# The first projection of a hybrid decoder trunk, issued in written order with the norm applied at eviction

## The chip, the cores and the metric

The kernel runs on one core of one Trainium2 chip. The metric is the device time of one execution in microseconds (us); three runs of the kernel before gave 558.02, 559.24 and 559.66 us, so the median is 559.24. The engines are named as the profile names them: PE (matrix multiplications, with PEld for its weight loads), DVE (element by element work, also the only one here that subtracts), ACT (functions, casts and scaled copies), POOL (memsets here) and SP, whose queue issues nearly every DMA.

## The reference, cut to what matters

Two layers, each of this form (x is 256 tokens by 1024):

```
for layer in range(2):
    h = rmsnorm(x, pre_norm[layer])            # x * rsqrt(mean(x*x) + eps) * g
    proj = h @ w_in[layer]                     # 1024 x 7704
    (hq, hf, hi, hz, nq, kc, vc, ks, vs, kw, vw, ng, nz) = split(proj)
    o_h = rmsnorm(hgrn2(hq, hf, hi), ...) * silu(hz)
    o_n = nsa(rope(nq), kc, vc, ks, vs, kw, vw, ng) * silu(nz)
    x = x + rmsnorm(concat(o_h, o_n) @ w_out[layer], post_norm[layer])
```

Only the start of layer 0 matters here: the norm of x, the product with the 1024 columns that give nq (the attention queries, scaled and rotated), and the handing over of the normalised x to the products that follow.

## The kernel before

**Precision.** Each float32 matrix is split into a high part (rounded to the fp32r type by an ACT cast) and a low part (DVE: the value minus its high part). A product is three matmuls: high by high, high by low, low by high.

**Tiles and units.** The tokens are two tiles of 128 (a = 0, 1). x is turned (transposed by PE, four 128x128 blocks per PSUM bank) so that the 1024 inputs lie on partitions in eight blocks; Hhi and Hlo hold its two parts. The weights come in units of 512 KB: one DMA into `raw` (five buffers), one ACT cast into `whi` (line 202), one DVE subtraction into `wlo` (line 203), eight buffers each. `Ring` issues the DMAs ahead of use; a DMA has to wait until the `raw` buffer that it writes has been read by line 203. Here w0, w1, ... are the units in the order of the plan. Units w0 to w7 make up the nq projection, w8 to w11 the next one (the forget gate of the first four heads, by `b_group`), and so on: w30 belongs to the third of the later groups (`kv_s`).

**The nq projection (a_pair, mm_a).** For each unit and each tile PE does six matmuls of 128x512: with weights of w and Hhi (line 368), w low and Hhi (369), w high and Hlo (370). The column group g = 0 uses w0 to w3, g = 1 uses w4 to w7. Tile 1 follows tile 0 by four units in layer 0. Three PSUM banks (`mmb`) hold the sums. When a sum is complete, `nq_evac` scales and rotates it (`rope`: one ACT op, four small DVE ops), and some microseconds later `turn_q` transposes the result (line 430).

**The norm (norm_in).** Per tile: ACT squares two halves of x (line 339), DVE adds the sums (341), ACT takes the root (331), DVE the reciprocal (332), DVE multiplies x by 1/rms and by g (344, g spread over the partitions by matmuls against a row of ones, line 1088), PE transposes (351), ACT and DVE split (355, 356).

**The order of work.** The instructions are recorded in program order and then placed on each engine by a scheduler; the functions given to `later` run when a counted PE time has passed, conversions of weights LAG = 9 us after their DMA is recorded. `consts2` loads the small constants (masks, biases, positions) and works out the forget gate's lower bound; before, it stands ahead of the layers. Each engine runs its instructions in order, each waiting for what it reads.

Of the kernel before, what the change touches and what calls it, by code (L numbers as in the profile page):

```python
# [10 lines left out]
F32 = mybir.dt.float32  # L11
# [84 lines left out]
def build(ctx, tc, A, out):  # L96
# [97 lines left out]
    class Ring:  # L194
        def __init__(self):
            self.made, self.taken, self.used = [], 0, 0
            self.split, self.lag = [], 0.0

        def convert(self, n):
            while len(self.split) < n:  # L200
                raw, hi, lo, shaped = self.made[len(self.split)]
                S.copy(out=hi, in_=raw)  # L202
                V.tensor_tensor(out=lo, in0=raw, in1=hi.bitcast(F32), op=OP.subtract)  # L203
                self.split.append((shaped(hi), shaped(lo)))

        def fill(self, n=RING):
            while len(self.made) < min(len(plan), self.used + n):
# [14 lines left out]
                if len(dims) == 3:  # L222
                    for a in range(dims[1]):
                        nc.sync.dma_start(out=shaped(raw)[:, :, a, :], in_=src[:, :, a, :])
                else:
                    nc.sync.dma_start(out=shaped(raw), in_=src)
                self.made.append((raw, hi, lo, shaped))
                if self.lag:
# [41 lines left out]
    def consts():  # L270
        nc.sync.dma_start(out=ct, in_=A["ct"])

    def consts2():
        rows = sp.tile([128, 128], F32, name="rows", tag="st", bufs=2)
        prow = sp.tile([128, 128], F32, name="prow", tag="st", bufs=2)
        m2 = sp.tile([128, 256], F32, name="m2", tag="st", bufs=2)
        nc.sync.dma_start(out=m2, in_=A["ct2"])
        nc.gpsimd.memset(cm3, 0.0)
        nc.gpsimd.memset(rows, 0.0)
# [6 lines left out]
        nc.gpsimd.memset(pat.rearrange("p (b t) -> p b t", t=32)[:, :, 0:1], 1.0)  # L286
        for i, nm in enumerate(("cmp_b1_k", "cmp_b1_v", "hgrn_out_norm")):
# [84 lines left out]

    def mm_b(ps, un, u, c):
# [49 lines left out]
    def nq_evac(a, g, ps):  # L423
        st = sp.tile([128, 4, 128], F32, name="st", tag="st", bufs=2)
        rope(st, ps.rearrange("p (h d) -> p h d", h=4), rope_q[a], 4, SCALE)
# [648 lines left out]

    def layers(general):
        ring = Ring()
        lm = None
        if not general:
            V.memset(eps_t, EPS)
            S.activation(out=eps_w, in_=eps_t, func=AF.Sqrt)  # L1080
        grow = slot("B0")[0:1, :D]
        ones = slot("B4")[0:1, 0:128]
        V.memset(ones, 1.0)
        nc.sync.dma_start(out=grow, in_=A["pre_norm"][0:1, :])
        xr = load_x(0, (0,), 2)
        gpre = [mmb(), mmb()]
        for q in range(2):
# [87 lines left out]
```

## Time and profile before

| | |
|---|---|
| median of 3 runs | 559.24 us |
| the profiled execution | 558.97 us |
| its span (first to last instruction) | 557.2 us |
| PE busy | 543.8 us (98%) |
| DVE busy | 398.8 us (72%) |
| ACT busy | 333.0 us (60%) |
| mean DMA rate | 173 GB/s |

The span is what the views below show; about 1.8 us of the execution lie around it. The busy times are shares of the whole span, so they say little of its first 40 us, which the change touches. A row of the timeline gives the start, the duration, the engine, the line of the kernel, the operation with the tile written and the tile read, its shape, and in square brackets how long the engine idled before it and which work ended that. Matmuls are pipelined: their pace is the distance of two starts, not the duration.

### The profile page before, as it was taken

To read this page: it belongs to the slowest core of one execution; us is meant where nothing else is said; L and a number is where in the kernel's file an instruction comes from. 1 tells how busy PE (TensorE), PEld (TensorE's weight loads), DVE (VectorE), ACT (ScalarE), POOL (GpSimd) and SP (SyncE) were. 2 spreads that over 40 slices of the span, in tenths; PEclk is the share of its full clock that TensorE was granted. 3 is DMA by queue.
4 is the path that set the end of the run, shared out by engine and by line. 5 is a ranking of instruction groups with operands and counts; after the bars stand their busy time and mean duration, and the time that the engine had idled before them with its cause. 6 is when DMAs were issued, how large, how long until landed. Compare 5 with 4: busy or idle time off the path is not lost.

```text
span 557.2 us, 9821 instructions
## 1 busy us (share of the span) xinstructions
PE 543.8 (98%) x3675; PEld 487.6 (88%) x3675; DVE 398.8 (72%) x883; ACT 333.0 (60%) x632; POOL 9.6 (2%) x18
## 2 busy tenths in 40 slices
PE   7999999999999999999999999989999999999994
PEld 4889998899888989988888999979988888898884
DVE  4887997889777277563687599888987654866422
ACT  6576537865567685562557763677646768746311
POOL 4000000000000001001000000000000000000000
PEclk9999999999999999999999999999999999999998
DMA  8698548965146158566385755697433622956111
GB/s 302 195 314 257 146 127 266 304 193 152 39 117 190 35 166 291 185 191 188 115 262 162 228 154 152 196 302 256 125 101 84 174 85 63 303 172 200 59 38 44
DMA packets 72197, 96.56 MB, mean 173 GB/s; under 512 B 3383, under 2 KB 49357, under 8 KB 72142
## 3 DMA queue, kind: packets, MB, share of 16 engines
q1 hardware_dynamic: 71854, 95.33, 55.2%
q8 instruction: 31, 0.51, 0.4%
q10 hardware_dynamic: 288, 0.52, 0.2%
q14 instruction: 24, 0.20, 0.1%
HBM read 93.75 MB, written 2.10 MB: 172 GB/s over the span
## 4 chain that ended last, share of the span: by engine, by line
PE 88%; DMA 4%; ACT 3%; DVE 2%; issue 1%; SPq 0%; ACTq 0%; DVEq 0%
PE ps_mm L378 10%; PE ps_mm L380 10%; PE ps_mm L379 10%; PE ps_mm L368 9%; PE ps_mm L369 9%; PE ps_mm L370 9%; PE ps_mm L1005 4%; PE ps_mm L1007 4%; PE ps_mm L1006 4%; DMA raw<-in_w_in 2%; ACT whi L202 2%; PE ps_t L668 2%; DMA raw<-in_cmp_w_v 2%; PE ps_s L608 1%; DVE wlo L203 1%
## 5 line engine op out<-in xcount | busy, mean ns | idle before, releaser
L203 DVE TENSOR_TENSOR wlo<-raw,whi 128x1024 fp32r<-128x1024 f32 (+1 forms) x168 | 203.0, 1223 | 60.7 <-ACT whi L202 56.3
L202 ACT CAST whi<-raw 128x1024 fp32r<-128x1024 f32 (+1 forms) x168 | 174.9, 1052 | 87.9 <-PE ps_mm L379 24.5
L378 PE MATMUL ps_mm<-Hhi,whi 128*128 128x256 f32 x448 | 127.5, 285 | 0.0
L380 PE MATMUL ps_mm<-Hhi,wlo 128*128 128x256 f32 x448 | 125.7, 281 | 0.0
L379 PE MATMUL ps_mm<-Hlo,whi 128*128 128x256 f32 x448 | 125.7, 281 | 0.0
L368 PE MATMUL ps_mm<-whi,Hhi 128*128 128x512 f32 (+1 forms) x256 | 102.0, 399 | 0.7 <-ACT Hhi L355 0.7
L370 PE MATMUL ps_mm<-whi,Hlo 128*128 128x512 f32 (+1 forms) x256 | 98.9, 386 | 0.0
L369 PE MATMUL ps_mm<-wlo,Hhi 128*128 128x512 f32 (+1 forms) x256 | 98.8, 386 | 0.0
L379 PEld LDWEIGHTS ps_mm<-Hlo,whi 128*128 128x128 f32 x448 | 84.5, 189 | 0.1
L378 PEld LDWEIGHTS ps_mm<-Hhi,whi 128*128 128x128 f32 x448 | 84.3, 188 | 0.1
L380 PEld LDWEIGHTS ps_mm<-Hhi,wlo 128*128 128x128 f32 x448 | 84.4, 188 | 0.0
L370 PEld LDWEIGHTS ps_mm<-whi,Hlo 128*128 128x128 f32 x256 | 48.7, 190 | 10.3 <-DVE Hlo L356 0.3
L368 PEld LDWEIGHTS ps_mm<-whi,Hhi 128*128 128x128 f32 x256 | 48.9, 191 | 8.5 <-ACT Hhi L355 1.1
L369 PEld LDWEIGHTS ps_mm<-wlo,Hhi 128*128 128x128 f32 x256 | 49.0, 191 | 7.5 <-DVE wlo L203 0.5
L630 ACT ACTIVATE sB<-ps_s,nm 128x256 f32<-128x256 f32 (+1 forms) x40 | 16.9, 428 | 12.2 <-DVE nm L627 11.5
L627 DVE CUSTOM_DVE_ANT_0 ps_s<-ps_s,cm 128x128 f32<-128x128 f32 (+1 forms) x64 | 22.4, 371 | 1.9 <-PE ps_s L610 0.7
L671 DVE TENSOR_TENSOR sB<-ps_t,sB 128x512 fp32r<-128x512 f32 x12 | 8.3, 688 | 20.1 <-ACT sB L670 20.1
L1005 PE MATMUL ps_mm<-whi,sN 128*128 128x512 f32 x48 | 19.0, 397 | 0.0
L1006 PE MATMUL ps_mm<-wlo,Hhi 128*128 128x512 f32 x48 | 18.9, 395 | 0.0
L1007 PE MATMUL ps_mm<-whi,Hlo 128*128 128x512 f32 x48 | 18.9, 395 | 0.0
L1006 PE MATMUL ps_mm<-wlo,sN 128*128 128x512 f32 x48 | 18.9, 394 | 0.0
L1007 PE MATMUL ps_mm<-whi,sN 128*128 128x512 f32 x48 | 18.9, 394 | 0.0
(299 smaller groups left out, 921.0 us busy)
## 6 DMA issues: line engine op xcount, KB each, us to landing
raw<-in_w_in SPq DMA_DIRECT2D x112, 512.0 KB, 4.5
raw<-in_w_out SPq DMA_DIRECT2D x32, 512.0 KB, 4.3
raw<-in_w_in SPq DMA_DIRECT2D x8, 536.0 KB, 4.1
raw<-in_cmp_w_k SPq DMA_DIRECT2D x16, 256.0 KB, 3.4
raw<-in_cmp_w_v SPq DMA_DIRECT2D x16, 256.0 KB, 3.2
sB<-in_x SPq DMA_DIRECT2D x3, 512.0 KB, 3.6
sB<-in_post_norm SPq DMA_DIRECT2D x2, 512.0 KB, 4.8
xs<-sB SPq DMA_DIRECT2D x4, 256.0 KB, 2.0
```

Of the source, the lines that this page charges most:

```text
L202: S.copy(out=hi, in_=raw)
L203: V.tensor_tensor(out=lo, in0=raw, in1=hi.bitcast(F32), op=OP.subtract)
L368: P.matmul(out=ps, lhsT=hh, rhs=wh, start=k == 0, stop=False)
L369: P.matmul(out=ps, lhsT=hh, rhs=wl, start=False, stop=False)
L370: P.matmul(out=ps, lhsT=hl, rhs=wh, start=False, stop=k == KT - 1)
L378: P.matmul(out=ps, lhsT=wh, rhs=hh, start=k == 0, stop=False)
L379: P.matmul(out=ps, lhsT=wh, rhs=hl, start=False, stop=False)
L380: P.matmul(out=ps, lhsT=wl, rhs=hh, start=False, stop=k == KT - 1)
L627: V.tensor_tensor_reduce(out=sb[b], in0=sb[b], in1=mk[b], scale=-1.0, scalar=3e38, op0=OP.add, op1=OP.min, accum_out=nm[:, i, b:b + 1])
L1005: P.matmul(out=ps, lhsT=hi, rhs=wh, start=first, stop=False)
L1006: P.matmul(out=ps, lhsT=hi, rhs=wl, start=False, stop=False)
L1007: P.matmul(out=ps, lhsT=lo, rhs=wh, start=False, stop=last)
```

## The change

The nq projection of layer 0 gets a function of its own, `first`, whose instructions stay on each engine in the order in which they are written.

- x is turned as it comes from memory. DVE multiplies it by g, which now lies one value per partition (`gcol`, turned from an 8x128 load), while it copies it out of PSUM (`whole`); ACT makes the high part (`top`), DVE the low part (`rest`).
- The sum of squares is taken later (`squares`), and 1/rms is applied to the finished sums: `stats` puts it into the table and the scale that `nq_evac` uses.
- For the later projections x needs the factor too: `spread` multiplies the turned x by 1/rms (spread along the tokens by a matmul of ones with a diagonal) and splits it again into Hhi and Hlo.
- Each unit is used by both tiles, one after the other; the last pair of matmuls of most units is the one with the low part of x.
- The first conversions are cut in halves; w0 and the x of tile 1 are loaded in two DMAs each; the first columns of the constants (the identity) and g are loaded by ACT's queue.
- PE multiplies zeros (`dummies`, 384 columns of bf16) eight times ahead of the first transposes and twice behind them.
- `consts2` moves behind the first forget gate group; its two transposes and small DVE operations come later.

```diff
     class Ring:
+        def high(self, i, s=slice(None)):
+            raw, hi, lo, shaped = self.made[i]
+            S.copy(out=hi[:, s], in_=raw[:, s])
+
+        def low(self, i, s=slice(None)):
+            raw, hi, lo, shaped = self.made[i]
+            V.tensor_tensor(out=lo[:, s], in0=raw[:, s], in1=hi[:, s].bitcast(F32), op=OP.subtract)
...
     def consts():
-        nc.sync.dma_start(out=ct, in_=A["ct"])
...
+        nc.sync.dma_start(out=ct[:, 128:], in_=A["ct"][:, 128:])
...
+    def mm_x(ps, un, u, H, order):
+        last = (u == KT // 2 - 1, order[-1], 1)
+        for j, kind in enumerate(order):
+            for i in range(2):
+                k = 2 * u + i
+                P.matmul(out=ps, lhsT=H[kind[0] == "l"][:, k, :], rhs=un[kind[1] == "l"][:, i, :],
+                         start=(u, j, i) == (0, 0, 0), stop=(True, kind, i) == last)
...
+    def first(ring, general):
...
+        def dummies(n):
+            if not general:
+                for i in range(n):
+                    P.matmul(out=wps[:, 0:384], lhsT=cm3[:, 0:128], rhs=cm3, start=True, stop=True)
...
+        def whole(a, k0, n):
+            ks, o = slice(k0, k0 + n), (k0 % 4) * 128
+            V.tensor_tensor(out=full[a][:, ks, :],
+                            in0=turned[a, k0 // 4][:, o:o + 128 * n].rearrange("p (k t) -> p k t", k=n),
+                            in1=gcol[:, ks, None].to_broadcast([128, n, 128]), op=OP.mult)
+
+        def top(a, k0, n):
+            S.copy(out=H[a][0][:, k0:k0 + n, :], in_=full[a][:, k0:k0 + n, :])
...
+        def stats(a, ss):
+            r = rstd_of(ss[:, 0:1], D, 1, "r1")
...
+            def spread():
+                rb = tb()
+                P.matmul(out=rb[:, 0:128], lhsT=ones, rhs=rd, start=True, stop=True)
+                V.tensor_tensor(out=full[a], in0=full[a], in1=rb[:, None, 0:128].to_broadcast([128, 8, 128]),
+                                op=OP.mult)
+                S.copy(out=Hhi[:, a], in_=full[a])
+                V.tensor_tensor(out=Hlo[:, a], in0=full[a], in1=Hhi[:, a].bitcast(F32), op=OP.subtract)
...
+            ring.fill(4)
...
+            dummies(8)
+            gp = sb_()
+            P.transpose(out=gp[:, 0:8], in_=grow, identity=ident[0:8, 0:8])
+            V.tensor_copy(out=gcol, in_=gp[:, 0:8])
+            turn_x(0)
+            dummies(2)
...
+            unit(0, 0)
+            turn_x(1)
+            ring.high(1)
+            ring.low(1)
+            ring.fill(7)
+            unit(0, 1)
+            ring.high(2)
+            whole(1, 0, 4)
+            top(1, 0, 4)
+            rest(0, 4, 4)
+            rest(1, 0, 4)
+            whole(1, 4, 4)
+            top(1, 4, 4)
+            ring.low(2)
+            ring.fill(8)
+            rest(1, 4, 4)
+            unit(1, 0, late)
+            unit(1, 1, late)
+            ring.high(3)
+            ring.low(3)
+            unit(0, 2, late)
+            done()
+            unit(1, 2, late)
+            s0 = squares(0)
+            ring.high(4)
+            ring.low(4)
...
+            spread = [stats(0, s0), stats(1, s1)]
+            evacuate(0, 0)
+            ring.high(6)
+            ring.low(6)
...
     def layers(general):
...
+            if l == 0:
+                first(ring, general)
+            else:
+                a_pair(ring, nq_evac, 8)
...
                     rests.append(hgrn_fast(l, c, ring))
+                    if (l, c) == (0, 0):
+                        consts2()
```

How the change moves instructions, at three places. The first is PE at the start of the program. Before (L1088 spreads g, L351 transposes the normalised x of tile 0, L368 to L370 are the matmuls of w0):

```order
L1088 MATMUL ps_mm<-sB_97,sB_98 128x512 x2
L351 MATMUL ps_t<-ct,sA_121 128x128 x8
L368 MATMUL ps_mm<-whi,Hhi 128x512
L369 MATMUL ps_mm<-wlo,Hhi 128x512
L370 MATMUL ps_mm<-whi,Hlo 128x512
```

The same place now, behind the first eight dummies (sA_95 and sA_96 are the high and low part of tile 0, sA_97 that of tile 1, sB_116 its x):

```order
L1201 MATMUL ps_s<-ct,sB_102 128x8
L1116 MATMUL ps_t<-ct,sB_108 128x128 x8
L1110 LDWEIGHTS cm_71
L1110 MATMUL ps_o<-cm_71 128x384
L1110 LDWEIGHTS cm_71
L1110 MATMUL ps_o<-cm_71 128x384
L394 MATMUL ps_mm<-whi,sA_95 128x512 x2
L394 MATMUL ps_mm<-whi,sA_96 128x512 x2
L394 MATMUL ps_mm<-wlo,sA_95 128x512 x2
L1116 MATMUL ps_t<-ct,sB_116 128x128 x8
L394 MATMUL ps_mm<-whi,sA_95 128x512 x2
L394 MATMUL ps_mm<-whi,sA_96 128x512 x2
```

The matmuls of w0 for tile 0 now stand ahead of tile 1's transposes, and all of PE's queue behind those waits for the x of tile 1, then for w1.

The second place is SP's queue at the start, before:

```order
L1084 DMA sB0_97<-in_pre_norm 1x1024
L157 DMA sB2_101<-in_x 128x512 x2
L271 DMA ct_70<-in_ct 128x544
L226 DMA raw_109<-in_w_in 128x2x512
L226 DMA raw_115<-in_w_in 128x2x512
L157 DMA sB3_145<-in_x 128x1024
L226 DMA raw_147<-in_w_in 128x2x512
```

and now, down to the masks (raw_111 is w0, raw_119 is w1, raw_271 is w9, m2_610 holds the masks):

```order
L157 DMA sB2_108<-in_x 128x512 x2
L237 DMA raw_111<-in_w_in 128x512 x2
L157 DMA sB3_116<-in_x 128x512 x2
L239 DMA raw_119<-in_w_in 128x2x512
L239 DMA raw_123<-in_w_in 128x2x512
L286 DMA ct_70<-in_ct 128x416
L239 DMA raw_132<-in_w_in 128x2x512
...
L239 DMA raw_249<-in_w_in 128x4x256
L239 DMA raw_271<-in_w_in 128x4x256
L301 DMA m2_610<-in_ct2 128x256
```

x comes first, both halves of tile 1's x stand ahead of w1, the constants have moved behind w2, and the masks have moved behind w9 (before, they stood behind w7).

The third place is DVE between the low parts of w5 and w9. Before, w5 to w7, then the masks (L298 and L299 read them), then w8 and w9 followed each other:

```order
L203 TENSOR_TENSOR wlo<-raw,whi 128x1024 x3
L298 CAST mask_80<-m_209 128x128
L299 CAST cm_71<-m_209 128x128
L203 TENSOR_TENSOR wlo<-raw,whi 128x1024 x2
L295 CAST posh<-ps_t 128x128
```

Now there stand, behind w5 and the small operations of `stats`, from the end of the first eviction on (L417 ends an eviction, L314 and L315 read the masks, L1154 multiplies x by 1/rms, L1157 is its low part, L205 the low parts of w6, w7, w8 and w9, L459 those of the queries):

```order
L314 CAST mask_80<-m_610 128x128
L417 TENSOR_TENSOR st<-st,rt_312 128x4x32
L205 TENSOR_TENSOR wlo<-raw,whi 128x1024
...
L1154 TENSOR_TENSOR sN_99<-sN_99,ps_t 128x1024
L1157 TENSOR_TENSOR Hlo<-sN_99,Hhi 128x1024
L205 TENSOR_TENSOR wlo<-raw,whi 128x1024
L1154 TENSOR_TENSOR sN_100<-sN_100,ps_t 128x1024
L1157 TENSOR_TENSOR Hlo<-sN_100,Hhi 128x1024
L205 TENSOR_TENSOR wlo<-raw,whi 128x1024
L459 TENSOR_TENSOR qlo<-ps_t,q_380 128x512
L459 TENSOR_TENSOR qlo<-ps_t,q_388 128x512
L205 TENSOR_TENSOR wlo<-raw,whi 128x1024
```

Four operations of 1024 columns and both low parts of the queries have moved in ahead of the low part of w9, and the first eviction's last step stands behind an operation that waits for the masks.

## Rows read from the trace of the kernel before

**Rows 1.** The page, busy time of each engine (share of the span).

```profile
PE 543.8 (98%) x3675; PEld 487.6 (88%) x3675; DVE 398.8 (72%) x883; ACT 333.0 (60%) x632; POOL 9.6 (2%) x18
```

**Rows 2.** Waits of PE (total us, times, longest), whole span.

```profile
PE ps_mm L1088 <- DMA sB<-in_pre_norm: 2.2, 1, 2.2
...
PE ps_t L531 <- ACT whi L202: 1.4, 1, 1.4
```

**Rows 3.** Timeline of PE, first 17 us (start, us, engine, line, operation, shape).

```profile
2.25 3.75 PE L1088 MATMUL ps_mm<-sB,sB 1*128 1x512 f32 x4 [2.25 <-DMA sB<-in_pre_norm]
6.97 1.97 PE L351 MATMUL ps_t<-ct,sA 128*128 128x128 f32 x8 [0.98 <-DVE sA L344]
9.63 0.79 PE L368 MATMUL ps_mm<-whi,Hhi 128*128 128x512 f32 x1 [0.69 <-ACT Hhi L355]
...
11.61 0.63 PE L368 MATMUL ps_mm<-whi,Hhi 128*128 128x512 f32 x1
...
12.04 0.63 PE L369 MATMUL ps_mm<-wlo,Hhi 128*128 128x512 f32 x1
...
16.15 0.39 PE L370 MATMUL ps_mm<-whi,Hlo 128*128 128x512 f32 x1
...
16.38 0.39 PE L368 MATMUL ps_mm<-whi,Hhi 128*128 128x512 f32 x1
```

**Rows 4.** DMA moved per us from 0 to 40 us, 40 slices.

```profile
GB/s 0 4 227 302 287 222 371 379 424 393 408 408 406 414 363 354 227 358 264 295 84 126 371 32 0 32 57 162 358 387 353 358 374 383 368 347 123 216 316 159
```

**Rows 5.** SP's queue, timeline of its first issues.

```profile
0.73 0.34 SPq L1084 DMA_DIRECT2D sB<-in_pre_norm  x1
1.13 0.83 SPq L157 DMA_DIRECT2D sB<-in_x  x2
```

**Rows 6.** DMA issues of w1, two later units, the masks: KB, us to landing.

```profile
raw<-in_w_in SPq DMA_DIRECT2D x1, 512.0 KB, 6.4
...
raw<-in_w_in SPq DMA_DIRECT2D x2, 512.0 KB, 8.9
...
m<-in_ct SPq DMA_DIRECT2D x1, 128.0 KB, 4.6
```

**Rows 7.** Timeline of ACT, 3 to 22 us.

```profile
3.88 0.63 ACT L339 ACTIVATE sA<-sB 128x512 f32<-128x512 f32 x1 [1.66 <-DMA sB<-in_x]
...
4.62 0.63 ACT L339 ACTIVATE sA<-sB 128x512 f32<-128x512 f32 x1
...
8.05 1.05 ACT L202 CAST whi<-raw 128x1024 fp32r<-128x1024 f32 x1 [2.19 <-DMA raw<-in_w_in]
...
19.79 2.00 ACT L202 CAST whi<-raw 128x1024 fp32r<-128x1024 f32 x2
```

**Rows 8.** Timeline of DVE, 10 to 40 us.

```profile
10.27 1.28 DVE L356 TENSOR_TENSOR Hlo<-ps_t,Hhi 128x512 fp32r<-128x512 f32 x2
...
20.54 3.48 DVE L203 TENSOR_TENSOR wlo<-raw,whi 128x1024 fp32r<-128x1024 f32 x3
...
26.28 1.23 DVE L203 TENSOR_TENSOR wlo<-raw,whi 128x1024 fp32r<-128x1024 f32 x1 [0.85 <-ACT whi L202]
...
39.67 0.21 DVE L391 TENSOR_TENSOR st<-ps_mm,ct 128x64 f32<-128x64 f32 x1
39.80 0.21 DVE L392 TENSOR_TENSOR st<-ps_mm,ct 128x64 f32<-128x64 f32 x1
```

**Rows 9.** The chain that ended last, one piece (start, us, what).

```profile
37.42 0.44 PE ps_t L430 x4
```

**Rows 10.** Timeline of PE, first and thirteenth gate matmuls, then a kv_s one.

```profile
37.61 0.37 PE L378 MATMUL ps_mm<-Hhi,whi 128*128 128x256 f32 x1
...
39.37 0.28 PE L380 MATMUL ps_mm<-Hhi,wlo 128*128 128x256 f32 x1
...
91.23 0.40 PE L369 MATMUL ps_mm<-wlo,Hhi 128*128 128x512 f32 x1
```

**Rows 11.** Timeline of DVE, 87 to 92 us (w30 to w33).

```profile
87.27 4.62 DVE L203 TENSOR_TENSOR wlo<-raw,whi 128x1024 fp32r<-128x1024 f32 x4
```

**Rows 12.** Busy us of each engine from 0 to 88.43 us, five stretches summed.

```profile
sum 88.43, PE 84.51 PEld 75.54 DVE 72.17 ACT 53.70 POOL 5.93; mean PE 16.90 PEld 15.11 DVE 14.43 ACT 10.74 POOL 1.19
```

More of the change, by code (lines that the diff above doesn't have):

```diff
@@ L2 @@
 import numpy as np
-from contextlib import ExitStack
+from contextlib import ExitStack, nullcontext
 import concourse.bass as bass
@@ L196, in __init__, with fill @@
             self.made, self.taken, self.used = [], 0, 0
-            self.split, self.lag = [], 0.0
+            self.split, self.lag, self.early = [], 0.0, 0
+        def high(self, i, s=slice(None)):
[4 more added lines that the diff above has]
+            V.tensor_tensor(out=lo[:, s], in0=raw[:, s], in1=hi[:, s].bitcast(F32), op=OP.subtract)
         def convert(self, n):
             while len(self.split) < n:
-                raw, hi, lo, shaped = self.made[len(self.split)]
-                S.copy(out=hi, in_=raw)
-                V.tensor_tensor(out=lo, in0=raw, in1=hi.bitcast(F32), op=OP.subtract)
+                i = len(self.split)
+                if i >= self.early:
+                    self.high(i)
+                    self.low(i)
+                raw, hi, lo, shaped = self.made[i]
                 self.split.append((shaped(hi), shaped(lo)))
-        def fill(self, n=RING):
+        def fill(self, n=RING, parts=1):
             while len(self.made) < min(len(plan), self.used + n):
@@ L224, in fill @@
                         nc.sync.dma_start(out=shaped(raw)[:, :, a, :], in_=src[:, :, a, :])
+                elif parts > 1:
+                    for i in range(dims[0]):
+                        nc.sync.dma_start(out=shaped(raw)[:, i], in_=src[:, i])
                 else:
@@ L270, in consts, with clear @@
     def consts():
-        nc.sync.dma_start(out=ct, in_=A["ct"])
[L273 to L279, printed above, removed]
+        nc.sync.dma_start(out=ct[:, 128:], in_=A["ct"][:, 128:])
+    def clear():
         nc.gpsimd.memset(ATt, 0.0)
@@ L286, in consts2 @@
         nc.gpsimd.memset(pat.rearrange("p (b t) -> p b t", t=32)[:, :, 0:1], 1.0)
+    def consts2():
+        rows = small([128, 128], "rows", 1)
+        prow = small([128, 128], "prow", 1)
+        m2 = small([128, 256], "m2", 1)
+        nc.sync.dma_start(out=m2, in_=A["ct2"])
+        nc.gpsimd.memset(rows, 0.0)
         for i, nm in enumerate(("cmp_b1_k", "cmp_b1_v", "hgrn_out_norm")):
@@ L1077, in layers @@
         lm = None
[L1078 to L1087, printed above, removed]
-            P.matmul(out=gpre[q], lhsT=ones, rhs=grow[:, q * 512:(q + 1) * 512], start=True, stop=True)
         if general:
@@ L1093, in layers @@
             V.tensor_copy(out=lm, in_=lf)
-        else:
-            consts()
-        ring.fill(2)
-        norm_in(xr[0], 0, gpre, "A1", 0)
-        xr += load_x(0, (1,), 1)
-        ring.fill(4)
-        norm_in(xr[1], 1, gpre, "A3", 0)
-        ring.fill()
-        ring.lag = LAG
-        if not general:
-            consts2()
         for l in range(DEPTH):
-            a_pair(ring, nq_evac, 8 if l else 4)
+            if l == 0:
+                first(ring, general)
+            else:
+                a_pair(ring, nq_evac, 8)
             rests = []
```

116 lines of the change are left out of this document (114 added, 2 removed).

## The prediction

> **What bounds the kernel now.** I read the page's busy times first: PE works in 98% of the span [rows 1]. A share over 557 us says little of one stage, so the next view is PE's waits: five waits in the whole span, the two longest 2.2 us at the start and 1.4 us much later [rows 2]. Once PE has begun, its queue sets the end, so whatever shifts PE in the first 40 us shifts the end by the same, unless a later wait takes it back.
>
> The third view is PE's timeline [rows 3]. The first matmul of the nq projection starts at 9.63 us, after the root, the reciprocal, the multiplication by 1/rms and eight transposes. [...] The fourth view is ACT and the DMA rate: w0 landed only at 8.05 us, and ACT had waited 2.19 us for it [rows 7], with the queues moving 222 to 424 KB per us from 3 us on [rows 4]. The last view sets DVE against PE: the low part of w9 was ready at 27.5 us [rows 8] and used at 39.37 us [rows 10], a lead of 11.9 us. DVE is far ahead of PE here, and that lead is what the change spends.
>
> **The change, part by part.** All sums stand against the profiled execution, 558.97 us (span 557.2), which lies 0.27 us under the median of the three runs; the same shift is put on the median.
>
> *Arrival of the weights.* The queue starts with x, not with pre_norm, so x leaves at 0.73 instead of 1.13 us [rows 5]: 0.4 us earlier. In front of w1's last byte lie 70 KB (identity and g), 524 (x, tile 0), 524 (w0), 524 (x, tile 1) and 524 (w1), 2167 KB in units of 1000 bytes. Adding up the slices of the rate [rows 4] gives that amount at 8.9 us, less 0.4 for the earlier start. The same sum for w1 before (1856 KB) gives 8.15 us, and it landed at about 9.4, issued just under 3 and landing 6.4 later [rows 6]: 1.2 us behind the sum. So w1 should land at about 9.7 us, and w0's halves, by the same way, at 5.9 and 7.0. These are estimates from a rate that dips to 222; I allow 0.9 us either way.
>
> *PE's start.* Removed: root, reciprocal, the two multiplications by 1/rms and g, all ahead of the transposes. Added ahead of the first matmul: the turned x times g and its split in pieces, which are done while w0 is on its way. The first matmuls can start at about 6.6 us and not 9.63. But the 12 matmuls of w0 and w1 for tile 0 cannot be finished before w1 is there: 9.7 + 1.05 (ACT's high part [rows 7]) + 1.2 (DVE's low part) = 12 us. Tile 1's first piece then takes 0.7 on DVE and 0.6 on ACT, so the dense run starts at 13.3 us. Left are 84 matmuls at 0.2335 us [rows 3], 19.6 us; eight transposes of `turn_q` at 0.11 us [rows 9], 0.9 us; two small matmuls for `spread`, some 0.4 us; and a wait of about 0.8 us at the fourth PSUM bank, since `unit(1, 4)` needs the bank that `evacuate(0, 0)` frees and three are there. Sum: 35.0 us for the first gate matmul. Before it stood at 37.61 [rows 10], with six more transposes done by then (four of `turn_q`, two of the constants: 0.66 us). On PE alone the change gains 37.61 - 0.66 - 35.0 = 1.9 us.
>
> *DVE's queue.* Removed per tile: two small operations, two multiplications and two low parts of 512 columns, about 3.1 us, 6.2 in all. Added: g's product in five pieces and the low parts in five, 2.7 us each; the reciprocals, scales, tables and diagonals, 1.3; x times 1/rms and its low part, four operations of 1024 columns at 1.16 [rows 8], 4.6; memsets and g's copy, 0.6. That is 12 us, 5.8 us more than before. And the order is now fixed, so DVE and ACT wait for each other. The chain from w1 on: at 10.8 us DVE starts the low part of w1 (1.16), then pieces of 0.64 [rows 8], 14.6 us. ACT then does, without a break, the last high part of x (0.5), w3, four squares at 0.74 [rows 7], w4 and w5, three casts at about 0.96: 21.2 us. DVE follows with the low parts of w5 to w9 (five at 1.16), the four operations of `spread` (4.6), two waits of 1.2 us in which ACT casts Hhi, the small operations (1.05 for `stats`, 1.8 for two evictions at 0.13 to 0.21 each [rows 8]) and the queries' low parts (1.3): 17.0 us, so the low part of w9 is ready at 38.2 us. PE wants it 14 matmuls of 256 columns (1.6 us) behind 35.0, at 36.6. PE therefore waits in two places, for w8 and for w9, 1.6 us together. Before, the matmul that reads it stood at 39.37; less the 0.66 us of transposes that is 38.7. Now it stands at 38.3. Of the 1.9 us gained on PE, 0.4 us are left.
>
> *The masks.* The masks are read between two steps of the first eviction. Their DMA stands behind that of w9, which waits until DVE has read w4's buffer, at about 20 us. I take issue at 20.5 us and landing at 24 to 24.2 us, when DVE is at the cast: 0 to 0.2 us. Before, the same DMA took 4.6 us [rows 6], which would be 1.1 us; two units took 8.9 us, which would make it 5 us. I take 0.1.
>
> *What costs nothing.* ACT gains about 2.3 us of casts and one table load (the exponential of `consts2` now lies between two sigmoid groups), but to 88 us it is busy in 53.7 of 88.4 us [rows 12], so other work hides it; without that cover it would be 3.6 us. The moved transposes of `consts2` cost PE the same later. Later on DVE is the engine to watch: w30's low part was ready at 88.43 us (the first of four from 87.27 [rows 11]) and was read at 91.23 [rows 10], a lead of 2.8 us. Up to there DVE was busy 72.2 us [rows 12] and idle 16.3. Now it has 5.8 us more to do and idles about 7.0 us ahead of w1 and 4.9 in waits up to 38 us: 72.2 + 5.8 + 11.9 = 89.9 us, 1.5 later than before and within the lead. No wait there, but only 1.3 us are left.
>
> **Sum.** -1.9 (PE) + 1.6 (waits for w8 and w9) + 0.1 (masks) = -0.2 us: 558.8 by the profiled execution, 559.0 by the median. What can be told from no change in this kernel is about 0.3%, 1.7 us.
>
> [...] The rows show PE at work from 2.25 us (one-row matmuls) and in eight transposes from 6.97, and still at 1.2 GHz at 12.04 [rows 3]. [...]
>
> **The rivals.**
> 1. *The full PE gain is kept.* If w1 lands earlier (by up to 0.9 us) or ACT and DVE run their chain with less waiting than I count, both shorten and PE's own sum decides: -1.9 us, with the earlier landing -2.8. For it: the wait for Hhi and the squares are my largest terms, and each is taken at full length. Against it: DVE's order holds whatever PE does. Time 556.4 to 557.3.
> 2. *The clock stays at 1.2 GHz until the dense run.* The eight dummies run from about 1.1 to 3.7 us (384 columns, 0.32 us each at that pace), transposes to 5.7, two dummies to 6.4, then PE is sparse up to 13.3. Before, the level rose 4.3 us after matmuls stood back to back from 11.61 us [rows 3]. By the same, it would rise at 17.6 to 20 us; each us at the lower level costs 0.45 us of PE: 1.9 to 3.0 us on 35.0. Then PE is ready at 36.9 to 38.0 and DVE's waits shrink to 0 or 1.2: shift 0 to +1.1 us. Time 559.2 to 560.3.
> 3. *Slower: the masks hold DVE in the first eviction.* Every further us that the masks need goes into DVE's chain behind it, which already sets the end: the low parts of w6 to w9, both `spread` products and the bank for `unit(1, 4)` stand behind that cast. At 4.6 us to landing the kernel is 0.8 us slower than before; from about 5.5 us it is slower by over 1.7; at 7 us it is +3.2. For it: 8.9 us did occur [rows 6]. Against it: by 20 us the queue holds only w8 and w9. Time 561 to 562.5.
>
> **How the numbers follow.** My forecast, DVE's chain takes back the gain (-1.2 to +1.2 us around 559.0): 0.48. Rival 1: 0.26. Rival 2: 0.13. Rival 3: 0.13. Faster by over 0.3% needs -1.7: nearly all of rival 1 and a little of the forecast, 0.28. Slower by over 0.3%: rival 3 and the end of rival 2, 0.18. Within: 0.54. The likeliest case's own range is 557.8 to 560.4; the range of 8 in 10 goes down to the middle of rival 1 and up to the start of rival 3, 556.6 to 561.2.
>
> **What would show it.** Right: PE's first 512-column matmul near 6.6 us, a dense run from about 13.3; DVE with hardly a gap from 21 to 38 us; PE waiting on the low parts of w8 and w9 at the first gate matmuls; the thirteenth gate matmul near 38.3. Wrong on the clock: starts 0.43 us apart beyond 14 us. Wrong on DVE: the first gate matmuls run through without a wait, or its lead over PE at 40 us is several us. Wrong on the masks: an idle stretch ahead of the mask cast in DVE's row. Wrong altogether: a new wait of PE behind 60 us, or the low part of w30 later than its matmul.

## The result, and the profile after

The changed kernel takes 564.88 us (median of 4 runs, 564.77 to 565.99) where the kernel before takes 559.01 us beside it: ratio 1.0114, 95% interval 1.0101 to 1.0127. It is slower by some 6 us, outside the range on record. The profiled execution has a span of 562.7 us, against 557.2. The first rows are the page's busy times and its clock row; the busy times answer to [rows 1], and the clock row is in tenths, 40 slices.

```profile
PE 544.9 (97%) x3686; PEld 488.2 (87%) x3686; DVE 404.1 (72%) x898; ACT 336.7 (60%) x637; POOL 9.3 (2%) x17
...
PEclk9979999999999999999999999999999999999998
```

PE's busy time is only 1.1 us longer and the span 5.5, so most of the loss is time in which PE stood still. The clock row has a 7 in its third slice, 28 to 42 us. The waits of PE (total us, times, longest), which answer to [rows 2], begin with a wait that the kernel before did not have:

```profile
PE ps_t L454 <- DVE sN L1154: 4.0, 1, 4.0
PE ps_mm L394 <- ACT whi L201: 2.3, 3, 0.8
PE ps_t L555 <- DVE kst L417: 1.4, 2, 0.9
```

Next PE's timeline, which answers to [rows 3] and [rows 10]. The numbers in front are start and us; the bracket is the idle time ahead of the row and what ended it.

```profile
6.50 0.50 PE L394 MATMUL ps_mm<-whi,sA 128*128 128x512 f32 x1 [0.71 <-ACT whi L201]
...
13.40 0.73 PE L394 MATMUL ps_mm<-whi,sA 128*128 128x512 f32 x2 [0.51 <-ACT sA L1126]
...
28.37 0.66 PE L454 MATMUL ps_t<-ct,st 128*128 128x128 f32 x4
33.06 1.09 PE L454 MATMUL ps_t<-ct,st 128*128 128x128 f32 x4 [4.04 <-DVE sN L1154]
...
41.70 0.28 PE L402 MATMUL ps_mm<-Hhi,whi 128*128 128x256 f32 x1
```

The start and the dense run came as predicted (6.6 and 13.3 us). Then the second four of the eight `turn_q` transposes wait 4.04 us, and the first gate matmul stands at 41.70 instead of 35.0. What PE waits for is in DVE's rows, which answer to [rows 8]:

```profile
24.83 0.23 DVE L314 CAST mask<-m 128x128 uint8<-128x128 f32 x1 [1.24 <-DMA m<-in_ct]
...
27.11 1.21 DVE L1154 TENSOR_TENSOR sN<-sN,ps_t 128x1024 f32<-128x1024 f32 x1
29.43 1.23 DVE L1157 TENSOR_TENSOR Hlo<-sN,Hhi 128x1024 fp32r<-128x1024 f32 x1 [1.11 <-ACT Hhi L1156]
30.57 1.22 DVE L205 TENSOR_TENSOR wlo<-raw,whi 128x1024 fp32r<-128x1024 f32 x1
31.70 1.21 DVE L1154 TENSOR_TENSOR sN<-sN,ps_t 128x1024 f32<-128x1024 f32 x1
...
37.51 1.21 DVE L205 TENSOR_TENSOR wlo<-raw,whi 128x1024 fp32r<-128x1024 f32 x1
```

`spread` (L1154) multiplies by a bank of tag t, and `turn_q` writes into a bank of the same tag, of which there are two. The first four transposes took the bank that the first multiplication gave back; the second four needed the bank of the second, which ends at 32.91 us. The transposes were placed by the matmuls around them; PE reaches the second four at 29.03 us, and the DVE operation that frees their bank ends 3.9 us later. Part of that is the masks' wait: DVE stood 1.24 us for them in the chain that leads to this operation. The granted clock shows the second half of the cost (busy us of PE, PEld, DVE, ACT, POOL, then PEclk, DMA share, GB/s):

```profile
30.00:32.00 2.00, 0.00 (x0) 0.00 (x0) 2.00 (x3) 0.34 (x1) 0.00 (x0) 0.96 0.13 34
32.00:34.00 2.00, 0.94 (x5) 0.97 (x6) 0.92 (x1) 1.05 (x2) 0.00 (x0) 0.50 0.46 88
...
38.00:40.00 2.00, 2.00 (x8) 1.58 (x8) 0.72 (x1) 0.00 (x0) 0.00 (x0) 0.83 0.84 257
40.00:42.00 2.00, 2.00 (x11) 1.63 (x11) 0.79 (x4) 1.44 (x3) 0.00 (x0) 1.00 0.81 250
```

PE was idle from 29.0 to 33.06 us; the clock fell to 0.50 near 32 us, before PE went on, and rose again between 38 and 40 us. At 0.50 the matmuls of 512 columns start 0.43 us apart (two from 34.80 to 35.66), at 1.00 they start 0.23 us apart (two from 40.77 to 41.23). From 33.06 PE needs 8.64 us for four transposes and 24 matmuls of 512 columns, which at the full level take 6.04 (24 times 0.2335 and four times 0.11): 2.6 us more. Without the wait and without the fall the first gate matmul would stand at 41.70 - 4.04 - 2.6 = 35.06. The shift against the kernel before is 4.09 us there, 5.00 at the first compress matmul (89.17 against 84.17) and 5.3 at 109 us, and stays so to the end.

### The profile page after: what moved, and what is told of

Read it like the earlier page. It is cut to its first block, busy times and chain, and to the rows that moved or that the text cites. A ratio compares the mean times of both kernels' runs of the same rounds, so it can differ in the third digit from the quotient of the medians.

```text
span 562.7 us, 9857 instructions
## 1 busy us (share of the span) xinstructions
PE 544.9 (97%) x3686; PEld 488.2 (87%) x3686; DVE 404.1 (72%) x898; ACT 336.7 (60%) x637; POOL 9.3 (2%) x17
## 4 chain that ended last, share of the span: by engine, by line
PE 80%; DVE 8%; DMA 5%; ACT 4%; issue 3%; SPq 0%; DVEq 0%; ACTq 0%
PE ps_mm L402 8%; PE ps_mm L403 8%; PE ps_mm L404 8%; PE ps_mm L384 7%; PE ps_mm L385 7%; PE ps_mm L386 7%; PE ps_mm L1029 4%; PE ps_mm L1031 4%; PE ps_mm L1030 4%; DVE wlo L205 4%; DMA raw<-in_w_in 3%; ACT whi L201 2%; PE ps_t L692 2%; PE ps_s L632 1%; PE ps_mm L394 1%
## 5 line engine op out<-in xcount | busy, mean ns | idle before, releaser
L205 DVE TENSOR_TENSOR wlo<-raw,whi 128x1024 fp32r<-128x1024 f32 (+2 forms) x169 | 203.1, 1216 | 58.1 <-ACT whi L201 55.4
L201 ACT CAST whi<-raw 128x1024 fp32r<-128x1024 f32 (+2 forms) x169 | 174.7, 1047 | 78.5 <-PE ps_mm L403 17.5
L384 PE MATMUL ps_mm<-whi,Hhi 128*128 128x512 f32 (+1 forms) x224 | 88.0, 393 | 0.0
L385 PE MATMUL ps_mm<-wlo,Hhi 128*128 128x512 f32 (+1 forms) x224 | 85.0, 379 | 0.0
L386 PE MATMUL ps_mm<-whi,Hlo 128*128 128x512 f32 (+1 forms) x224 | 85.0, 379 | 0.0
L384 PEld LDWEIGHTS ps_mm<-whi,Hhi 128*128 128x128 f32 x224 | 42.2, 188 | 6.1 <-issue 0.4
L385 PEld LDWEIGHTS ps_mm<-wlo,Hhi 128*128 128x128 f32 x224 | 42.3, 189 | 5.5
L394 PE MATMUL ps_mm<-whi,sA 128*128 128x512 f32 x64 | 20.4, 431 | 2.9 <-ACT whi L201 2.3
L1029 PE MATMUL ps_mm<-whi,sN 128*128 128x512 f32 x48 | 19.0, 396 | 0.0
L1029 PE MATMUL ps_mm<-whi,Hhi 128*128 128x512 f32 x48 | 18.9, 394 | 0.0
```

The costliest lines, as they stand in the source:

```text
L201: S.copy(out=hi[:, s], in_=raw[:, s])
L205: V.tensor_tensor(out=lo[:, s], in0=raw[:, s], in1=hi[:, s].bitcast(F32), op=OP.subtract)
L384: P.matmul(out=ps, lhsT=hh, rhs=wh, start=k == 0, stop=False)
L385: P.matmul(out=ps, lhsT=hh, rhs=wl, start=False, stop=False)
L386: P.matmul(out=ps, lhsT=hl, rhs=wh, start=False, stop=k == KT - 1)
L394: P.matmul(out=ps, lhsT=H[kind[0] == "l"][:, k, :], rhs=un[kind[1] == "l"][:, i, :], start=(u, j, i) == (0, 0, 0), stop=(True, kind, i) == ...
```

## The experiments

The first question was whether the bank and the clock are the whole loss, and the first runs said no. The second was where the rest is. The runs are told in that order; those with the same number in the table's first column ran in one session with the kernel before, whose median was 558.4 to 558.9 us.

| session | kernel | us | ratio to before, 95% interval |
|---|---|---|---|
| 1 | e1_banks | 562.88 | 1.0067 (1.0043 to 1.0090) |
| 1 | e2_fill | 563.35 | 1.0085 (1.0063 to 1.0107) |
| 1 | e3_turnlate | 561.12 | 1.0036 (1.0014 to 1.0058) |
| 1 | e4_nodummies | 561.58 | 1.0047 (1.0023 to 1.0070) |
| 2 | e5_late_consts | 559.32 | 1.0009 (0.9989 to 1.0029) |
| 2 | e6_early_consts | 562.21 | 1.0051 (1.0032 to 1.0069) |
| 2 | e7_ahead | 560.13 | 1.0020 (1.0001 to 1.0038) |
| 2 | e8_ahead_nodummies | 561.72 | 1.0045 (1.0025 to 1.0065) |
| 3 | e9_more_vector | 560.19 | 1.0029 (1.0003 to 1.0054) |
| 3 | e10_pool | 559.64 | 1.0010 (0.9984 to 1.0036) |
| 3 | e11_pool_between | 558.97 | 0.9999 (0.9976 to 1.0022) |
| 3 | e12_changed_again | 565.59 | 1.0107 (1.0066 to 1.0148) |
| 4 | e13_before_gpsimd | 563.65 | 1.0086 (1.0057 to 1.0115) |
| 4 | e14_between_gpsimd | 562.41 | 1.0075 (1.0049 to 1.0101) |
| 5 | e15_before_less_vector | 556.69 | 0.9952 (0.9935 to 0.9969) |
| 5 | e16_between_less_vector | 554.15 | 0.9916 (0.9894 to 0.9937) |

**The bank, the clock, the place of the transposes.** e1_banks gives the two `spread` matmuls banks of other tags:

```diff
-                rb = tb()
+                rb = sb_() if a else ob()
```

> Changed kernel with one edit: the two small matmuls of spread write the idle banks 'o' and 's' instead of the two 't' banks. Theory A (the second group of query transposes waits 4.0 us because both 't' banks are held until DVE has multiplied by 1/rms, and the idle stretch drops the clock to 1.2 GHz up to 38.8 us): the 4.04 us wait in front of the query transposes at 33.06 us is gone, no matmul start is 0.43 us apart after it, the first gate matmul starts near 35.1 us instead of 41.70, PE then waits some 1.1 us for the low part of w8 and 1.2 us for that of w9 (ready at 38.7), total 564.9 - 4.7 = 560.2 us. Rival B (DVE's longer queue is the loss, and PE would stand still whichever banks are used): PE's waits only move to the gate matmuls and further waits follow up to 90 us, total 563 us or more.

e2_fill leaves the wait and keeps PE at work in it, with 25 dummy matmuls between the two groups of transposes:

```diff
-            tick(LQ)
+            clock[0] += LQ
+            heapq.heappop(heap)[3]()
+            dummies(25)
+            tick(0.0)
```

> Changed kernel with one edit: 25 more multiplications of zeros (384 columns) between the two groups of query transposes, so that PE works while the second group's bank is not free. The wait itself stays. Theory A, clock part: the second group still starts at about 33.1 us, but the following 24 matmuls run 0.23 us apart and not 0.43, first gate matmul near 39.1 instead of 41.70, total 564.9 - 2.6 = 562.3 us. If the lower clock has another cause than the idle stretch: matmuls still 0.43 us apart behind it, total 564.9 us.

e3_turnlate writes the transposes behind the last unit of tile 0:

```diff
-            tick(LQ)
             unit(0, 6, late)
...
             unit(0, 7, late)
             done()
+            tick(LQ)
             evacuate(0, 1)
```

> Changed kernel with one edit: both groups of query transposes are issued behind the matmuls of w7 for tile 0 (in front of the third eviction) instead of in front of those of w6; banks as in the changed kernel. Theory A: PE reaches them at about 33 us, when both 't' banks are free, so no wait and no lower clock; the low part of w9 no longer stands behind the queries' low parts if DVE's order follows. Total 559.5 to 560.5 us. Rival B: no gain, 563 us or more.

PE's timeline in e2_fill:

```profile
28.59 0.60 PE L454 MATMUL ps_t<-ct,st 128*128 128x128 f32 x4
29.03 4.23 PE L1110 MATMUL ps_o<-cm 128*128 128x384 bf16 x25
33.09 0.60 PE L454 MATMUL ps_t<-ct,st 128*128 128x128 f32 x4
...
39.10 0.28 PE L402 MATMUL ps_mm<-Hhi,whi 128*128 128x256 f32 x1
```

The wait is still there, filled, and PE stays at its full pace: the four transposes and 24 matmuls take 6.01 us from 33.09; the first gate matmul comes at 39.10 instead of 41.70. So the fall of the clock is worth 2.6 us at that place, as worked out above, and the place without the wait is 39.10 - 4.06 = 35.04. In e1_banks neither is left, and the gate does start at 35.40:

```profile
35.40 0.28 PE L402 MATMUL ps_mm<-Hhi,whi 128*128 128x256 f32 x1
...
36.61 0.38 PE L404 MATMUL ps_mm<-Hhi,wlo 128*128 128x256 f32 x1 [0.75 <-DVE wlo L205]
...
38.94 0.38 PE L404 MATMUL ps_mm<-Hhi,wlo 128*128 128x256 f32 x1 [0.64 <-DVE wlo L205]
```

There are also the two waits for the low parts of w8 and w9 that the prediction had, 1.4 us together instead of 1.6. Yet at the end e1_banks has won back only about 2.3 of 6.6 us and e2_fill about 1.2 of 2.6 (ratios against 1.0107 in e12_changed_again, below, times 558.5; against the 1.0114 of the result it is 2.6 and 1.6). The intervals are 1.2 us or more on either side, so e1_banks is clearly short of 6.6, and e2_fill is not clearly short of 2.6: its profiled execution, at 562.31 us one of its faster ones, keeps all of it (span 560.2 against 562.7). All three medians came out above what I expected. The waits of PE in e1_banks show where the rest went:

```profile
PE ps_t L555 <- DVE kst L417: 2.6, 2, 1.5
PE ps_mm L404 <- DVE wlo L205: 1.4, 2, 0.8
PE ps_s L516 <- ACT gt L611: 1.2, 1, 1.2
```

Against the kernel before, PE in e1_banks is 0.4 us late at 84 us, 1.9 behind the wait at L516 (the bank of the gates and values: `gt` on ACT stands behind `vlo` on DVE), 2.4 behind the key transposes at 105 us and 2.8 at 140. The loss had moved from 30 to between 84 and 140 us, but for some 0.9 us behind 350 us, in layer 1. Of the 2.6 us at the transposes of the compressed keys (L555, L531 in the kernel before, called key transposes here), 1.13 are in layer 0 and 1.50 in layer 1. The kernel before waits at both places too, 0.61 and 1.40 us; its list puts the second down to ACT, so it stands in another line of [rows 2]:

```profile
103.44 0.26 PE L531 MATMUL ps_t<-ct,kst 15*128 15x15 f32 x2 [0.61 <-DVE kst L393]
372.33 0.27 PE L531 MATMUL ps_t<-ct,kst 15*128 15x15 f32 x2 [1.40 <-ACT whi L202]
```

The 2.0 us of such waits that the expectations of e13 and e15 below name are these two together; only 0.61 of them lies at 85 to 105 us. In the changed kernel itself those waits were mostly hidden by PE's own lateness. e3_turnlate did better than e1_banks: there the low parts of w9 and w10 stand ahead of the queries' low parts on DVE, and its wait at L516 is 0.6 us.

**The dummies.** e4_nodummies is e1_banks without the ten dummy matmuls, e8_ahead_nodummies the same for e7_ahead below.

> The kernel with the idle banks (first run of this list) without any of the ten multiplications of zeros. Theory of the prediction (the early clock is hidden behind DVE's chain unless it stays low beyond 16 us): matmuls 0.43 us apart up to 17.6 to 20 us, PE ready for the gate matmuls at 37 to 38 instead of 35.1 us, waits for w8 and w9 shrink to about nothing, total 0 to 1.1 us above the first run of this list. If the clock rises without them by 14 us: equal within 0.3 us. If the early clock is worth its full price: 2 to 3 us above.

> e7_ahead without any of the ten dummy matmuls. If the dummies cost nothing and give the early clock: 0 to 0.5 us slower than e7_ahead. If the 1.3 us by which e4_nodummies was under e1_banks is theirs: 1 us faster than e7_ahead.

One came out 1.3 us under its pair, the other 1.6 us over it. The intervals of both pairs overlap, and the signs differ: these times do not tell what the dummies are worth. The traces tell a little more: without dummies the first gate matmul is at 35.18 us in e4_nodummies (35.40 in e1_banks) and at 36.24 in e8_ahead_nodummies (35.20 in e7_ahead). In e4_nodummies matmuls stand 0.23 us apart from 13.5 us on, earlier than the 17.6 us of rival 2.

**The constants and the conversions.** Between 50 and 80 us DVE is busy nearly all the time, in the kernel before (29.5 of 30 us) as in e1_banks (20.0 of the 20 us from 55 on), so two causes were open: the constants' small operations, which the change moved into that stretch, or conversions of weights that run behind. This is the view of the conversion's line alone on DVE, from 0 to 40 us, in the kernel before (another view than [rows 8]), in e1_banks and in e11_pool_between; the count is in brackets.

```profile
0.00:40.00 40.00, 16.98 (x15) 1.00 0.82 268
```

```profile
0.00:40.00 40.00, 12.67 (x12) 1.00 0.69 226
```

```profile
0.00:40.00 40.00, 15.97 (x14) 1.00 0.77 253
```

By 40 us the kernel before has made 15 low parts and e1_banks 12. e5_late_consts moves only the constants, in the kernel before; e6_early_consts puts them back into the head of e1_banks:

```diff
-            consts2()
+            clear()
...
                     rests.append(hgrn_fast(l, c, ring))
+                    if (l, c) == (0, 0):
+                        consts2()
```

> The kernel before, with one part of the change alone: the constants (masks, rows of biases, positions and bounds, their two transposes and some 20 small vector operations) are loaded and worked out behind the first scan group, as in the changed kernel, instead of ahead of the first projection. Theory A: with VectorE busy without a gap from about 50 to 85 us, the 2 us of small operations and the exponential's two table loads come out at its end as waits of PE for the key/value rows: 1 to 2 us slower than before (559.5 to 560.5). Rival B: the loss of the changed kernel past 40 us is only that its conversions run behind (12 weight units converted at 39 us where the kernel before has 16); then this one is within 0.5 us of before, since its conversions are as early as they were.

> The changed kernel with the spread matmuls in banks of their own (as e1_banks) and the constants worked out in the gaps of the first projection again. Theory A: about 2 us less than e1_banks, 560.5 to 561.2; the waits of PE at the gate's matmul (L516 of the changed kernel) for ACT goes. Rival B (late conversions): 562.5 or more, with the same waits as e1_banks.

Both give little: 0.5 us over before, with an interval on both sides of no change, and 0.9 us under e1_banks by the ratios, inside their intervals. Theory A of these two, 1 to 2 us, is not borne out; the place of the constants is a small part at most. e7_ahead is e6 with the order changed, so that DVE has a conversion to make where it stood 1.1 us for ACT:

```diff
+            ring.high(7)
             spread[0][0]()
+            ring.low(7)
...
+            ring.high(8)
             spread[0][1]()
             spread[1][0]()
+            ring.low(8)
...
+            ring.high(9)
             spread[1][1]()
+            ring.low(9)
```

> e6_early_consts with the conversions of w7, w8, w9 written ahead of the low parts that wait for ACT, so that VectorE does not stand 1.1 us twice, and tile 1's transposed x evicted ahead of w1's low part. If late conversions are the other half of the loss: no wait of PE at the low parts of w8 and w9, the first gate matmul at 34.5 to 35, and 557 to 558.5, at or under the kernel before. If they cost nothing: as e6_early_consts within 0.5.

It is 2.1 us under e6, though 1.6 over my upper end. No wait for w8 and w9 is left, and the gate starts at 35.20; 2.8 us at the key transposes (1.33 of them in layer 0) and 1.2 at the gates' bank are still there, and they take the lead back: against the kernel before, PE in e7_ahead is 2.0 us early at 80 us, 1.6 at 82, 0.2 behind the gates, and 0.6 late behind the keys at 104 us.

**VectorE's load.** e9_more_vector tests the other way round: the kernel before, and nothing but vector work added.

```diff
-            V.tensor_tensor(out=lo, in0=tp, in1=hi.bitcast(F32), op=OP.subtract)
+            for _ in range(3 if len(turns) <= 4 else 1):
+                V.tensor_tensor(out=lo, in0=tp, in1=hi.bitcast(F32), op=OP.subtract)
```

> The kernel before with vector work added and nothing else: each of the four conversions of turned queries in layer 0 (between 33 and 45 us) makes its low part three times instead of once, 8 more subtractions of 0.69 us, about 5 us, which is what the changed kernel adds on VectorE in the first 40 us (10.6 us of evictions, spread and low parts against 5.6 us). Theory A, VectorE's lead is what is lost: 2 to 4 us slower than before (560.5 to 562.5), with new waits of PE at the transposes of keys (L531) and the gate. Rival B, VectorE has slack there and the loss past 40 us is from something else (the DMA queue, ACT): within 0.5 us of before.

It is 1.6 us slower by the ratio (0.2 to 3.0), at the low end of what I gave or under it, and PE waits at the place where e1_banks waits. These are e9's key transposes, in layer 0 and layer 1; 0.61 and 1.40 us in the kernel before:

```profile
103.75 0.26 PE L535 MATMUL ps_t<-ct,kst 15*128 15x15 f32 x2 [1.58 <-DVE kst L393]
373.86 0.27 PE L535 MATMUL ps_t<-ct,kst 15*128 15x15 f32 x2 [1.93 <-DVE kst L393]
```

Against the kernel before, PE in this execution loses 1.4 us between 50 and 105 us and another 1.2 in layer 1, where the edit adds nothing. So the first part is what the added vector work shows; the second is not explained by it.

The next two take small operations off DVE and PE's wait for w1's low part out of the way:

```diff
-                V.tensor_copy(out=KC[:, :, c0:c0 + 2], in_=pv.bitcast(F32))
+                nc.gpsimd.tensor_copy(out=KC[:, :, c0:c0 + 2], in_=pv.bitcast(F32))
...
-            unit(0, 1)
+            rest(1, 0, 4)
+            unit(0, 1, part=0)
+            unit(1, 0, late, part=0)
+            unit(0, 1, part=1)
+            unit(1, 0, late, part=1)
```

> e7_ahead with about 2 us of small vector operations of layer 0 (masks, positions into the key/value operand, the bounds' arithmetic but three operations, the block of ones) on GpSimd, which is idle there. Theory A: 1 to 2 us faster than e7_ahead (558.1 to 559.1), the waits at the key transposes and at the gate shorter. Rival B: as e7_ahead, 560.1.

> e10_pool with tile 1's first four matmuls of unit 0 ahead of tile 0's matmuls on the low part of w1, so that PE does not stand 1.1 us for it. If VectorE's lead decides past 50 us: as e10_pool within 0.5, since PE only arrives earlier at the same waits. If PE decides: 1 us faster than e10_pool.

e10 and e11 are each some 0.6 us under the one ahead, within their intervals; together with e7 they bring the changed kernel back to the time of the kernel before, not below it. In the profiled execution of e11, which at 557.08 us is the fastest of its 12 (the slowest took 561.53), the first gate matmul is at 33.36 us: 4.25 earlier than before, 3.8 with the four transposes fewer that were done by then. At 103 us 3.1 are left, and 3.0 at PE's last matmul (546.39 against 549.42); the rest of the execution behind it then takes 1.1 us longer, and the span is 1.9 shorter (555.3). Its waits (0.98 of the 1.8 us are in layer 0):

```profile
PE ps_t L568 <- DVE kst L430: 1.8, 2, 1.0
PE ps_o L1123 <- DVE eps_t L1207: 1.1, 1, 1.1
PE ps_s L1217 <- DMA sB<-in_pre_norm: 0.6, 1, 0.6
```

> The changed kernel itself, on the chip of these runs: 564 to 565.5 with before at 558.5 (ratio 1.010 to 1.0125); the same 4.0 us wait of PE for VectorE and the same stretch at half the granted clock.

This is e12_changed_again. It repeats the result; with the 4.0 us wait it also shows 1.2 us at L516.

**Less vector work in the stretch.** First I moved three multiplications of the scan to GpSimd, in the kernel before (e13) and in e11 (e14):

```diff
-            V.tensor_tensor(out=K, in0=K, in1=Q, op=OP.mult)
+            nc.gpsimd.tensor_tensor(out=K, in0=K, in1=Q, op=OP.mult)
```

> The kernel before with three multiplications of the scan (the keys' scaling, L797, 1.22 us, and the two of the lower keys, L811 and L814, 0.69 us each; two halves, two layers) on GpSimd instead of VectorE: 5.2 us of vector work out of 60 to 80 us, and as much in layer 1. Theory A (VectorE's lead decides the waits at the key transposes, 2.0 us in the kernel before): 1 to 2 us faster, 556.5 to 557.5. Rival B (those waits have another cause, or GpSimd slows VectorE by as much): within 0.5 us of before or slower.

> e11_pool_between with the same three multiplications on GpSimd. Theory A: 1 to 2.5 us faster than e11, its 1.8 us of waits at the key transposes gone: 556.5 to 558, under the kernel before and, if the earlier start of the dense part is now kept, 0 to 1.5 us under e13. Rival B: as e11, 559.

Both got slower, e13 by 4.8 us against before and e14 by 4.2, where e11 is level with it. GpSimd's and DVE's rows of e13 show where:

```profile
75.19 2.40 POOL L797 TENSOR_TENSOR sB<-sB,sB 128x1024 f32<-128x1024 f32 x1 [8.14 <-PE ps_mm L370]
```

```profile
74.97 0.60 DVE L478 TENSOR_TENSOR sN<-ps_mm,sN 128x256 fp32r<-128x256 f32 x1
75.47 3.20 DVE L203 TENSOR_TENSOR wlo<-raw,whi 128x1024 fp32r<-128x1024 f32 x1
```

The subtraction takes 3.20 us instead of 1.22: it finishes 1.1 us after GpSimd's multiplication, as if it had only then begun. In e14 the same subtraction, beside the same multiplication (75.43 to 77.80 us), takes 3.16 us and finishes 1.1 us after it as well. So e13 did not relieve DVE, it held it up. In this execution PE loses 1.8 us to that between 70 and 80 us, 0.9 at the key transposes of layer 0, and 2.5 us in layer 1. There it waits 1.73 us at the key transposes, and behind them the granted clock falls once more (columns as above):

```profile
378.00:380.00 2.00, 2.00 (x11) 2.00 (x10) 1.55 (x5) 1.15 (x2) 0.00 (x0) 0.50 1.01 337
```

In e14 PE waits 3.3 us for DVE at 76 us, with the clock at 0.50 behind it. e15 and e16 leave the same three multiplications out (the recurrence's output is then not the reference's) in the kernel before and in e11:

```diff
-        for i, f in enumerate((forward, ends, backward, scale, refs, lower_keys)):
+        for i, f in enumerate((forward, ends, backward, lambda: None, refs, lambda: None)):
```

> The kernel before, leaving out three multiplications of the scan (the keys' scaling and the two of the lower keys, L797, L811 and L814; the recurrence's output isn't the reference's): 5.2 us less of vector work between 60 and 80 us, and as much in layer 1, and nothing in its place. Theory A (VectorE's lead decides the waits of PE at 85 to 105 us, 2.0 us in all): 1.5 to 2.5 us faster than before. Rival B (they have another cause): within 0.5 us of before.

> e11_pool_between leaving out the same three multiplications. Theory A, and the earlier dense part is kept once VectorE has room: 1 to 2 us faster than e15 (3 to 4 us faster than before). If the earlier start is lost in another place (DMA, ACT): as e15 within 0.5.

The waits of PE at the key transposes, in e15 and, for e16, the longest entry of all:

```profile
PE ps_t L531 <- DVE kst L393: 0.4, 1, 0.4
```

```profile
PE ps_mm L407 <- ACT whi L201: 2.1, 3, 1.0
```

With room on DVE the kernel before is faster by 0.48% (2.7 us) and e11 by 0.84% (4.7 us) than the kernel before as it was. Behind the start no wait for DVE is left in e16's list, only three at the head for weights. Between the two, 0.36% or 2.0 us: that is what the earlier dense part is worth when VectorE has room. By the profiles e15 gains 0.7 us in layer 0, at the key transposes, and 1.0 at those of layer 1, which have nothing to do with the earlier start.

How much VectorE's load between 80 and 105 us takes back in the kernels that compute everything, the profiles show too: 2.6 us in e7, 1.2 in e10 and 0.7 in e11. So e7 loses its whole lead there, while the profiled execution of e11 keeps most of it. Why e11's median is no better than that of the kernel before is not shown.

## Why the prediction was wrong

*The step that failed* is the term "eight transposes of `turn_q` at 0.11 us, 0.9 us" in PE's start. I took their duration and no wait. The second four stand in the queue behind a bank that DVE gives back at 32.91 us: 4.04 us of idle time, and 2.6 us more since the clock fell in it. I had counted banks for `unit(1, 4)` and not for the tag that `spread` and `turn_q` share, although DVE's order, which I had worked out, gives the time of the second multiplication. 4.04 + 2.6 takes the first gate matmul from 35.06 to 41.70. The waits for w8 and w9, 1.6 us in the sum, did not come in their place because PE arrived after their low parts. The net at the gate is 4.09 us, and 4.75 with the six transposes that moved behind it.

*Right, with sizes:* w1 landed at 9.79 us (9.7 predicted), as this row of ACT shows, which answers to [rows 7]:

```profile
9.79 1.05 ACT L201 CAST whi<-raw 128x1024 fp32r<-128x1024 f32 x1 [1.53 <-DMA raw<-in_w_in]
```

The dense run began at 13.40 (13.3), and without the bank PE would have been ready at 35.06 (35.0). The low part of w9 was ready at 38.7 us (38.2). Inside the 35.0 one term was off: the wait of 0.8 us at the fourth bank was 0.2 in e2_fill; other small pieces made up for it. ACT's terms in DVE's chain add up to 20.9 and not to 21.2 us; the low part of w5 did start at 20.66. The matmul that first reads the low part of w9 is the fifteenth of the gate (39.37 us in the kernel before), not the thirteenth, as the prediction and [rows 10] call it; the sum had its place right. Once the bank was out of the way, the two waits for w8 and w9 did appear (1.4 us, e1_banks). Up to 40 us, then, the sum had one missing term.

*The masks* were mis-sized: DVE stood 1.24 us for them and not 0.1. The duration that the same DMA had before would have given 1.1 [rows 6]; I had that number and took the lower end. In the chain that ended last of the changed kernel the DMA takes as long as it did before:

```profile
20.17 4.63 DMA m<-in_ct
```

The 1.24 us are more than the half us by which w9's low part was late, so other pieces of DVE's chain were shorter than counted.

*The later part* was wrong as well, hidden in the changed kernel and seen in e1_banks. I tested one lead, that of w30, 2.8 us, and concluded that no wait comes of it. PE did not wait for w30. It waited for the evictions between the conversions in the same DVE queue, the keys' rotation and the low part of the values, which had no lead at all: the kernel before waits 0.6 us for them already. That vector work costs time there is shown from both sides by the wait at the key transposes of layer 0: 0.61 us before, 1.58 with 5 us more (e9), none with 5.2 us less (e15). The whole times, +1.6 and -2.7 us, hold changes in layer 1 as well.

*The rivals.* Rival 1 (1.9 us or more kept) did not happen in the changed kernel; e16, with room on VectorE, keeps 2.0 us against e15. Rival 2 did not happen: the dense run from 13.40 us was at full pace (0.23 us apart from 13.97 on). The clock did cost 2.6 us, but at 33 us and because of a wait. The pace of the transposes differed too: eight of `turn_q` take 0.79 us from start to start in e1_banks at 28.97 us, and four take 0.74 us in the changed kernel at 33.06, with the clock at 0.50. Rival 3 had the sign, and the masks did hold DVE; but they landed after 4.63 us, at its own price of 0.8 us, and not after the 5.5 from which it was to decide.

*What stays open:* what the dummies are worth, and why e11's executions lie 4.5 us apart, since only the fastest has a profile. The granted clock differs along with such times: of the 31 executions of the kernel before in session 1 (556.47 to 562.39 us), the six that took 559.86 us or more have a mean granted clock of 0.992 or 0.993, the other 25 one of 0.995 or more. Whether the clock fell behind the key transposes of layer 1 in those six, as it did in the profiles of e3 and e13 (0.50 at 378 to 380 us), is not shown. How much of e1_banks' 3.7 us is DVE's order (e7 mends it) and how much its load (e15 and e16) is known only to about 1 us.

## What to carry to other kernels

When an order is written by hand, list for each instruction the buffer it writes and the last reader of that buffer, by tag and count of banks, before its duration; here one of 0.11 us held PE's queue for 4.04. Behind that idle stretch the matmuls at a granted clock of 0.50 cost another 2.6 us, so one of that length has to be priced with them; shorter ones may have to be, too: behind a wait of 1.7 to 1.9 us in layer 1 the clock fell (to 0.50) in the profiles of e3 and e13, and not in that of e9. And to say that an engine has a lead, take the shortest lead of everything in its queue, not that of one kind of item; where that is near zero, work added ahead can come out behind it, as 5 us more on VectorE cost PE 1.4 us by 105 us in e9.

## What the runs showed that I had not expected

A subtraction of 1024 columns took 3.20 us instead of 1.22 beside one multiplication on GpSimd, and moving 5.2 us of vector work per layer from VectorE to GpSimd made the kernel 4.8 us slower (e13). After the 4.04 us of idle time TensorE ran at half the clock for over 5 us of dense matmuls (0.50 from 32 to 38 us). The 1.2 GHz of the prediction and of e1's expectation is a pace, worked out from starts in the rows: 512 columns in 0.43 us are 1.19 columns per ns, against 2.19 at 0.2335 us; the views give the clock only as a share of full speed. And the clock of a stretch has to be set against the pace of its matmuls: in the kernel before, matmuls of 512 columns stand 0.43 us apart at 12 us [rows 3], while the view of the stretch gives a granted clock of 1.00, so the lower level at 12 us is one of pace, and why it was lower is not shown:

```profile
12.00:16.00 4.00, 4.00 (x11) 3.09 (x10) 3.51 (x6) 3.36 (x6) 0.00 (x0) 1.00 1.04 384
```
